# RMSNorm on one core: 19 transfers of x and out become 15, and two stores wait for a load

## The chip, the cores and the metric

The kernel runs on one core of a Trainium2 chip. The metric is the device time of one execution in microseconds (us), as the median of the runs. A profile of one execution shows what each engine did: PE (TensorE), DVE (VectorE), ACT (ScalarE), POOL (GpSimd), SP (SyncE, which here only issues transfers), and the core's 16 DMA engines.

## The reference

```
x: (16, 1024, 512) float32, gamma: (512,) float32
eps = 1e-5
rms = sqrt(mean(x ** 2, axis=-1, keepdims=True) + eps)
out = x / rms * gamma
```

Each of the 16,384 rows of 512 numbers is divided by its root mean square and multiplied by gamma. x has 33.55 MB and so has out; each byte crosses once.

## The kernel before

The rows are seen as 4 tiles of 128 partitions with 32 rows each (`xv`, `ov`: tile t, partition p, row r). One row over 128 partitions is 256 KB, one tile 8 MB. Three slots in SBUF hold a tile each: tiles 0 to 3 live in slots 0, 1, 2 and 0 again, so the loads of tile 3 overwrite rows of slot 0 that must have been stored. Results are written in place, into the slot.

A tile is worked in groups, `(tile, first row, rows, pieces of the squares, rows that POOL scales)`, listed in `groups` (L76). Tile 0 has three groups, (0,0) with 7 rows, (0,7) with 9 and (0,16) with 16; the others have two of 16. For each group:

- `square_sums` (L89): ACT squares a piece of rows into a scratch (L96), DVE sums each row of it (L97). A piece of 7 or 4 rows goes to PSUM (`sq_psum`), one of 5 to `sq_sbuf`. A piece of 9 rows goes to rows 23 to 32 of slot 2, which lie unused until tile 2 is loaded there.
- `inverse_rms` (L101): ACT takes the root (L102), DVE the reciprocal (L103).
- `scale_by_pool` (L106): POOL multiplies its share of the rows by the reciprocal (L109) and by gamma (L110).
- `scale` and `times_gamma` (L115, L120): for the other rows, ACT multiplies by the reciprocal, row by row (L118), and DVE by gamma (L122).

The main loop (L166) works one group ahead: the squares of the next group are recorded before the scaling of this one. The schedule is written by hand (`manual_schedule`): each engine runs its instructions in the order in which the code records them, and waits only where data demand it.

All transfers are issued by SP, in recorded order, to one queue: loads at L45, stores at L49, gamma at L58. An SP instruction that waits holds back all later ones. A transfer signals when it has landed. The first loads, of tile 0 and half of tile 1, are recorded ahead of the loop; the rest in `transfers` (L129), which is called after each group. Gamma is loaded in five pieces, spread over the partitions by a matmul (L66) and copied for POOL (L165).

The calls that the change touches stand after groups (0,0), (0,16) and (1,16). After (0,0), for instance, rows 0 and 1 of tile 0 are stored one at a time, between them the second half of tile 1 is loaded, and then rows 0 to 23 of tile 2, the part of slot 2 that holds no scratch. Rows 23 to 32 of tile 2 are loaded after (0,16), when the scratch has been read for the last time, by group (1,0), whose pieces are 7 and 9.

Of the kernel before, what the change touches and what calls it, by code (L numbers as in the profile page):

```python
# [9 lines left out]
def kernel(  # L10
# [15 lines left out]
    N, D = xf.shape  # L26
# [17 lines left out]
    def load(t, slot, r0, r1):  # L44
        dma = nc.sync.dma_start(out=slots[slot][:, r0:r1], in_=xv[t][:, r0:r1])  # L45
        before_scale.append((slot, r0, r1, dma))

    def store(t, slot, r0, r1):
        dma = nc.sync.dma_start(out=ov[t][:, r0:r1], in_=slots[slot][:, r0:r1])  # L49
        before_scale.append((slot, r0, r1, dma))  # L50

    gamma_row = const.tile([1, D], fp32)
    pieces = (0, 128, 224, 320, 416, D)

    load(0, 0, 0, 1)
    load(0, 0, 1, 8)
    for c0, c1 in zip(pieces, pieces[1:]):
        nc.sync.dma_start(out=gamma_row[:, c0:c1], in_=gamma.unsqueeze(0)[:, c0:c1])  # L58
    load(0, 0, 8, 16)
    load(0, 0, 16, 32)  # L60
    load(1, 1, 0, 16)

    ones_col = const.tile([1, P], fp32)
    nc.gpsimd.memset(ones_col, 1.0)  # L64
# [12 lines left out]
        (0, 0, 7, (7,), 3),  # L77
        (0, 7, 9, (9,), 5),
        (0, 16, 16, (7, 9), 7),
        (1, 0, 16, (7, 9), 7),  # L80
        (1, 16, 16, (7, 5, 4), 7),
        (2, 0, 16, (7, 5, 4), 7),
        (2, 16, 16, (7, 5, 4), 7),
# [36 lines left out]
    def times_gamma(t, g, r0, r1):  # L120
# [4 lines left out]
        for slot, b0, b1, earlier in before_scale:  # L125
            if slot == slot_of[t] and b0 < g + r1 and g + r0 < b1:
                tc.declare_no_dep(scaled.ins, earlier.ins, reason="ScalarE waited for it before it scaled these rows")

    def transfers(t, g):  # L129
        if (t, g) == (0, 0):  # L130
            store(0, 0, 0, 1)
            load(1, 1, 16, 32)
            store(0, 0, 1, 2)
            load(2, 2, 0, 23)
        elif (t, g) == (0, 16):
            store(0, 0, 2, 3)
            load(2, 2, 23, 32)
            store(0, 0, 3, 16)
            store(0, 0, 16, 32)
            load(3, 0, 0, 16)  # L140
            load(3, 0, 16, 32)
        elif (t, g) == (1, 16):
            store(1, 1, 0, 32)
        elif (t, g) == (2, 16):
            store(2, 2, 0, 32)
        elif (t, g) == (3, 0):
            store(3, 0, 0, 16)
        elif (t, g) == (3, 16):
            store(3, 0, 16, 32)
# [16 lines left out]
    for k, group in enumerate(groups):  # L166
        t, g, n, pieces, share = group
        mine = n - share
        half = (mine + 1) // 2
        ahead = groups[k + 1 :][:1]  # L170
        ss, todo = pieces_of(ahead[0]) if ahead else (None, [])
        scale_by_pool(rstd, t, g, n, share)
        for piece in todo[:2]:
            square_sums(*piece)
        scale(rstd, t, g, 0, half)
        for piece in todo[2:]:
            square_sums(*piece)
        scale(rstd, t, g, half, mine)
        times_gamma(t, g, 0, mine)
        transfers(t, g)  # L180
        for nxt in ahead:
            rstd = inverse_rms(ss, nxt[2])
# [30 lines left out]
```

## Time and profile before

| | before |
|---|---|
| median of 3 runs | 161.58 us (161.57 to 161.96) |
| profiled execution, span from first to last instruction | 160.2 us |
| bytes moved, mean rate over the span | 67.12 MB, 419 GB/s |
| busy DVE / ACT / POOL | 112.0 / 107.8 / 106.4 us |
| transfer engines busy | 98.1% of the span |
| end of the last compute instruction (DVE, L122) | 139.1 us |
| issue of the last store | 139.2 us |

The span is what the profile sees of one execution; a run's time is longer by what lies around it, 1.4 us here against the median. Busy times are sums over the span and say nothing of who waits for whom. Transfers are read in two ways: by the time from issue to landing, which holds the wait behind earlier transfers in the queue, and by the distance of two landings, which does not.

### The profile page before, as it was taken

Reading aid. Unit: us, or ns where it says so; the run is one execution under the profiler, and the core shown is the slowest. Engines: PE = TensorE matmul, PEld = TensorE weight load, DVE = VectorE, ACT = ScalarE, POOL = GpSimd, SP = SyncE. Lnnn points to the kernel's source line nnn. Section 1 sums busy time; section 2 is a strip of 40 time slices with the busy share of each in tenths; the row PEclk is TensorE's granted clock in tenths of the full one; section 3 lists DMA queues with packets and bytes.
Section 4 is the critical chain, followed back from the end, with each engine's and each line's share of the span. In section 5 each row is a group of like instructions: output and inputs, shape, how many; then the busy total and the mean of one; then the engine's idle time right before and its main releaser. Section 6 shows DMA issues by size and latency. Waiting matters only on the chain.

```text
span 160.2 us, 276 instructions
## 1 busy us (share of the span) xinstructions
PE 2.0 (1%) x2; PEld 0.5 (0%) x2; DVE 112.0 (70%) x39; ACT 107.8 (67%) x108; POOL 106.4 (66%) x24
## 2 busy tenths in 40 slices
PE   0050000000000000000000000000000000000000
PEld 0010000000000000000000000000000000000000
DVE  0018098899798999999999999999999009700000
ACT  3071967976999998999899899989960990000000
POOL 1000951994999599999999999999999980000000
DMA  5999999899999899999999999996996996999994
GB/s 189 431 421 475 442 401 458 340 446 491 417 435 494 388 379 383 426 450 475 434 401 426 483 401 393 524 491 295 524 491 295 524 491 295 401 491 417 401 450 196
DMA packets 2747, 67.12 MB, mean 419 GB/s; under 512 B 313, under 2 KB 314, under 8 KB 826
## 3 DMA queue, kind: packets, MB, share of 16 engines
q1 hardware_dynamic: 2746, 67.11, 98.1%
q14 instruction: 1, 0.01, 0.0%
HBM read 33.56 MB, written 33.55 MB: 419 GB/s over the span
## 4 chain that ended last, share of the span: by engine, by line
DVE 59%; ACT 22%; DMA 4%; ACTq 0%; issue 0%; SPq 0%
DVE ss L97 36%; DVE slot L122 23%; ACT slot L118 8%; ACT slot L96 7%; ACT sq_psum L96 6%; DMA slot<-in_x_dram 4%; DVE ss L103 1%; ACT ss L102 1%; ACTq L208 0%; ACT gamma_b L165 0%; SPq L45 0%; ACTq L96 0%
## 5 line engine op out<-in xcount | busy, mean ns | idle before, releaser
L109 POOL TENSOR_TENSOR slot<-slot,ss 128x3584 f32<-128x3584 f32 (+2 forms) x9 | 47.0, 5218 | 24.1 <-DVE ss L103 24.1
L110 POOL TENSOR_TENSOR slot<-slot,gamma_b 128x3584 f32<-128x3584 f32 (+2 forms) x9 | 59.3, 6587 | 0.7
L97 DVE TENSOR_REDUCE ss<-sq_psum 128x7 f32<-128x3584 f32 (+1 forms) x13 | 42.2, 3247 | 13.7 <-ACT sq_psum L96 13.7
L118 ACT ACTIVATE slot<-slot,ss 128x512 f32<-128x512 f32 x75 | 47.3, 706 | 4.7 <-DVE ss L103 4.7
L122 DVE TENSOR_TENSOR slot<-slot,gamma_psum 128x4608 f32<-128x4608 f32 (+2 forms) x9 | 41.3, 4590 | 8.7 <-ACT slot L118 8.7
L96 ACT ACTIVATE sq_psum<-slot 128x3584 f32<-128x3584 f32 (+1 forms) x13 | 34.6, 2658 | 6.4 <-DMA slot<-in_x_dram 5.7
L97 DVE TENSOR_REDUCE ss<-slot 128x9 f32<-128x4608 f32 x3 | 14.9, 4954 | 4.4 <-ACT slot L96 4.2
L97 DVE TENSOR_REDUCE ss<-sq_sbuf 128x5 f32<-128x2560 f32 x5 | 14.0, 2803 | 0.0
L96 ACT ACTIVATE slot<-slot 128x4608 f32<-128x4608 f32 x3 | 12.1, 4033 | 0.0
L96 ACT ACTIVATE sq_sbuf<-slot 128x2560 f32<-128x2560 f32 x5 | 11.6, 2321 | 0.0
L102 ACT ACTIVATE ss<-ss,eps_t 128x16 f32<-128x16 f32 (+2 forms) x9 | 2.7, 305 | 11.9 <-DVE ss L97 11.9
L103 DVE RECIPROCAL ss<-ss 128x16 f32<-128x16 f32 (+2 forms) x9 | 2.1, 236 | 0.4 <-ACT ss L102 0.4
L66 PE MATMUL gamma_psum<-gamma_row,ones_col 1*128 1x512 f32 x2 | 2.0, 1122 | 8.6 <-DMA gamma_row<-in_gamma_dram 8.6
L72 ACT ACT_TABLE_LOAD x1 | 1.3, 1283 | 1.2 <-PEq L197 1.2
L165 ACT COPY gamma_b<-gamma_psum 128x512 f32<-128x512 f32 x1 | 0.6, 567 | 0.0
L66 PEld LDWEIGHTS gamma_psum<-gamma_row,ones_col 1*128 1x128 f32 x2 | 0.5, 308 | 8.6 <-issue 8.6
L64 POOL MEMSET ones_col<- 1x128 f32 x1 | 0.2, 195 | 0.3 <-POOLq L197 0.3
L197 POOL MEMSET const-float32-0.0<- 128x1 f32 x1 | 0.1, 99 | 0.2 <-issue 0.2
L72 ACT ACTIVATE table<-eps_t 128x1 f32<-128x1 f32 x1 | 0.2, 202 | 0.0
L197 POOL MEMSET const-bfloat16-1.0<- 128x1 bf16 x1 | 0.1, 102 | 0.0
L197 POOL MEMSET const-uint8-127<- 128x1 uint8 x1 | 0.1, 102 | 0.0
L197 POOL MEMSET const-float32-1.0<- 128x1 f32 x1 | 0.1, 99 | 0.0
(1 smaller groups left out, 0.1 us busy)
## 6 DMA issues: line engine op xcount, KB each, us to landing
slot<-in_x_dram SPq DMA_DIRECT2D x5, 4096.0 KB, 21.9
out_dram<-slot SPq DMA_DIRECT2D x3, 4096.0 KB, 23.4
slot<-in_x_dram SPq DMA_DIRECT2D x1, 5888.0 KB
out_dram<-slot SPq DMA_DIRECT2D x1, 3328.0 KB, 21.8
slot<-in_x_dram SPq DMA_DIRECT2D x1, 2304.0 KB, 14.3
slot<-in_x_dram SPq DMA_DIRECT2D x1, 2048.0 KB, 9.9
slot<-in_x_dram SPq DMA_DIRECT2D x1, 1792.0 KB, 7.0
out_dram<-slot SPq DMA_DIRECT2D x3, 256.0 KB
```

What stands on the lines that cost most here:

```text
L66: nc.tensor.matmul(gamma_psum[:, 0], ones_col, gamma_row, start=True, stop=True)
L72: nc.scalar.activation(out=table, in_=eps_t, func=AF.Sqrt)
L96: nc.scalar.activation(out=sq[:, :m], in_=rows, func=AF.Square)
L97: nc.vector.tensor_reduce(out=ss[:, r : r + m, 0], in_=sq[:, :m], axis=mybir.AxisListType.X, op=OP.add)
L102: nc.scalar.activation(out=ss[:, :n, 0], in_=ss[:, :n, 0], func=AF.Sqrt, bias=eps_t, scale=1.0 / D)
L103: nc.vector.reciprocal(out=ss[:, :n, 0], in_=ss[:, :n, 0])
L109: nc.gpsimd.tensor_tensor(out=part, in0=part, in1=by_row, op=OP.mult)
L110: last = nc.gpsimd.tensor_tensor(out=part, in0=part, in1=gamma_b.to_broadcast([P, share, D]), op=OP.mult)
L118: nc.scalar.activation(out=x[:, g + r, :], in_=x[:, g + r, :], func=AF.Copy, scale=rstd[:, r])
L122: scaled = nc.vector.tensor_tensor(out=part, in0=part, in1=gamma_psum.to_broadcast([P, r1 - r0, D]), op=OP.mult)
L165: nc.scalar.copy(out=gamma_b[:, 0], in_=gamma_psum[:, 0])
L197: nc = _bacc.Bacc("TRN2", target_bir_lowering=False, num_devices=1)
```

## The change

The one-row stores of tile 0 go, and loads and stores are cut differently:

| | before | after |
|---|---|---|
| tile 0 in | rows 0:1, 1:8, 8:16, 16:32 | 0:8, 8:32 |
| gamma | 5 pieces | 1 piece |
| tile 1 in | 0:16 at the start, 16:32 after (0,0) | 0:16, 16:32, both at the start |
| tile 2 in | 0:23 after (0,0), 23:32 after (0,16) | 0:30, 30:32, both after (0,7) |
| tile 0 out | 0:1 and 1:2 after (0,0), 2:3, 3:16, 16:32 after (0,16) | 0:16, 16:32 after (0,16) |
| tile 3 in | 0:16, 16:32 | 0:16, 16:30, 30:32 |
| tile 1 out | 0:32 | 0:32 |
| tile 2 out, tile 3 out | 0:32; 0:16, 16:32 | the same |

Two stores get a wait that their data do not ask for: tile 0's rows 0:16 are issued when the load of tile 2's rows 0:30 has landed, and tile 1's when the load of tile 3's rows 16:30 has. The squares of group (1,0) are cut into pieces of 7, 5 and 4 rows in place of 7 and 9; the last reader of the scratch in slot 2 is then group (0,16).

```diff
-    def store(t, slot, r0, r1):
+        return dma
+
+    def store(t, slot, r0, r1, behind=None):
         dma = nc.sync.dma_start(out=ov[t][:, r0:r1], in_=slots[slot][:, r0:r1])
+        if behind is not None:
+            tc.add_manual_dep(
+                dma.ins,
+                behind.ins.name,
+                mybir.DependencyInfo(mybir.DependencyClass.Sync, mybir.DependencyReason.DATA),
+                reason="the store is issued when this load has landed",
+            )
         before_scale.append((slot, r0, r1, dma))
...
-    pieces = (0, 128, 224, 320, 416, D)
+    pieces = (0, D)
 
-    load(0, 0, 0, 1)
-    load(0, 0, 1, 8)
+    load(0, 0, 0, 8)
     for c0, c1 in zip(pieces, pieces[1:]):
         nc.sync.dma_start(out=gamma_row[:, c0:c1], in_=gamma.unsqueeze(0)[:, c0:c1])
-    load(0, 0, 8, 16)
-    load(0, 0, 16, 32)
+    load(0, 0, 8, 32)
     load(1, 1, 0, 16)
+    load(1, 1, 16, 32)
...
-        (1, 0, 16, (7, 9), 7),
+        (1, 0, 16, (7, 5, 4), 7),
...
+    late = {}
+
     def transfers(t, g):
-        if (t, g) == (0, 0):
-            store(0, 0, 0, 1)
-            load(1, 1, 16, 32)
-            store(0, 0, 1, 2)
-            load(2, 2, 0, 23)
+        if (t, g) == (0, 7):
+            late[2] = load(2, 2, 0, 30)
+            load(2, 2, 30, 32)
         elif (t, g) == (0, 16):
-            store(0, 0, 2, 3)
-            load(2, 2, 23, 32)
-            store(0, 0, 3, 16)
+            store(0, 0, 0, 16, behind=late[2])
             store(0, 0, 16, 32)
             load(3, 0, 0, 16)
-            load(3, 0, 16, 32)
+            late[3] = load(3, 0, 16, 30)
+            load(3, 0, 30, 32)
         elif (t, g) == (1, 16):
-            store(1, 1, 0, 32)
+            store(1, 1, 0, 32, behind=late[3])
```

## The prediction

> **What bounds the kernel now.** I read the page's DMA rows first, because 67 MB pass through one core, then the SP rows of the timeline (every transfer is issued there), then the DMA issues with their time to landing, and last the chain of waits.
>
> The row of slices for the transfer engines, and the queue's row (packets, MB, share of 16 engines):
>
> ```profile
> DMA  5999999899999899999999999996996996999994
> ...
> q1 hardware_dynamic: 2746, 67.11, 98.1%
> ```
>
> One queue carries everything and its 16 engines hardly pause between the first and the last slice. DVE, ACT and POOL are busy 70, 67 and 66%. The last compute instruction (DVE, L122) ends at 139.1 and the span at 160.2, so 21 us at the end are transfers alone. The transfer engines are the bound: time is bytes at a fixed rate plus every pause of the queue. The chain view on the page names DVE for 59%, but it only follows the work that released the last store; that store waited behind others (20.1 us from issue to landing, of which its own data takes half).
>
> The SP rows of the timeline (start, length and number of issues):
>
> ```profile
> 0.74 0.86 SPq L45 DMA_DIRECT2D slot<-in_x_dram  x2
> ...
> 3.17 5.39 SPq L45 DMA_DIRECT2D slot<-in_x_dram  x3
> ...
> 28.69 0.43 SPq L45 DMA_DIRECT2D slot<-in_x_dram  x1
> ...
> 49.83 0.33 SPq L45 DMA_DIRECT2D slot<-in_x_dram  x1
> 50.25 5.48 SPq L49 DMA_DIRECT2D out_dram<-slot  x2
> 72.09 10.27 SPq L45 DMA_DIRECT2D slot<-in_x_dram  x2
> 83.64 55.90 SPq L49 DMA_DIRECT2D out_dram<-slot  x4
> ```
>
> and one row of SP's waits (total, times, longest):
>
> ```profile
> SPq L208 <- DMA out_dram<-slot: 19.6, 3, 9.6
> ```
>
> SP always issues well ahead of need. The first load of tile 2 is issued at 28.69, while loads issued before it land until 43.1 (completion events). The last 9.6 us wait is one 16-row store: a row of 128 partitions (256 KB) costs 0.604 us (completion events 149.67 and 159.34: 9.67 for 16 rows). 256 rows cost 154.7 us; the other 4.6 us before the last landing are start-up and small losses.
>
> Time to landing of three loads at the start (size, us):
>
> ```profile
> slot<-in_x_dram SPq DMA_DIRECT2D x1, 256.0 KB, 2.9
> ...
> slot<-in_x_dram SPq DMA_DIRECT2D x1, 1792.0 KB, 7.0
> ...
> slot<-in_x_dram SPq DMA_DIRECT2D x1, 4096.0 KB, 24.5
> ```
>
> They were issued at 0.74, 1.18 and 8.24 and landed at 3.6, 8.2 and 32.8. The last is 16 rows, 9.67 us of data, and took 24.5: it landed 9.95 after the load issued before it (22.83), so the queue serves in order of issue, one transfer after the other.
>
> And from the chain, the piece of it that the change will lean on:
>
> ```profile
> 16.20 3.95 ACT slot L96
> ...
> 25.47 3.04 ACT sq_psum L96
> 28.51 3.97 ACT slot L96
> ...
> 32.51 4.96 DVE ss L97
> ```
>
> From the start of the 9-row square of (0,7) at 16.20 to the end of the second 9-row reduce at 37.46 there are 21.26 us in which ACT and DVE wait for each other step by step, none of it for a transfer.
>
> **The change, part by part.** Times below are landings; the span ends 0.83 us after the last (159.34 to 160.17), and the median 161.58 is 1.41 above the span.
>
> *The price of a restart.* In the trace before, the queue runs dry only at the start, so that is the nearest row. Issue at 0.74, eight rows landed at 8.22: 7.48 less 8 x 0.604 leaves 2.65 us. That is the upper end, since it includes the one-row transfer's 2 KB packets (117 ns mean there, 84 ns in mid-run). Lower end: first packet at 1.75, so 1.0 after issue, and 0.35 from last packet to landing (158.99 to 159.34): 1.35, which is the quickest engine's case and not the slowest's. I take the middle, 2.0. Below 1.35 nothing can go, because both pieces are seen; a store may restart differently from a load, and no row shows it.
>
> The Trainium skill, "DMA: Bandwidth & Descriptors", section "Latency and other measured facts", gives about 0.6 us to the first byte for SP's path; by an estimate from that figure a restart would cost 0.95 and not 2.0, the first pause below 2.7 us, the other two nothing, and the sum would be 163.5. The trace's 1.0 us to the first packet differs from it, and the trace decides.
>
> *Load of rows 8 to 32 in one piece.* The 9-row square needs rows 8 to 16. Before, they had landed at 13.1 and the square began at 16.20. Now it waits for all 24 rows: x(0, 0:8) at about 7.8, plus 24 x 0.604, is 22.3. So the whole compute chain moves by 6.1 us.
>
> *Load of tile 2 moved past the scratch.* Before, rows 0 to 23 of slot 2 were loaded from 28.69, free of the scratch in rows 23 to 32. Now the load of rows 0 to 30 is issued after (0,7) and overwrites the scratch, so on SP it waits for the second 9-row reduce (the instruction order has it wait for DVE's seventh). That is 21.26 us after the square: 22.3 + 21.3 + 0.05 = 43.6. What is queued ahead by then: x(1, 0:16) and x(1, 16:32), 2 x 9.67 plus the 0.28 that the first of them lost before, so the queue is empty at 22.3 + 19.6 = 41.9. The load restarts it: 43.6 + 2.0 - 41.9 = **3.7 us of pause** (3.1 to 4.4). This does not depend on when the 24 rows land, as both sides start from it. Behind the waiting load on SP stand the 2-row load and the stores of tile 0; no engine waits for these in this time.
>
> *The stores behind a load.* The store of rows 0 to 16 used to be issued at 50.25 while loads ran until 64.1. Now SP holds it until x(2, 0:30) has landed; covered only by the two remaining rows, 1.21 us. Pause: 0.05 + 2.0 - 1.21 = 0.84 (0.2 to 1.5). The store of tile 1, before at 83.64 with some 17 us of loads ahead of it, waits the same way for x(3, 16:30): 0.84 again. **Together 1.7 us** (0.4 to 3.0). Its scale work is long done (POOL ends (1,16) at 83.6 before, 90 now; the landing is at 103). Behind it on SP is the store of tile 2, whose rows are done at 118, before 125 when the tile 1 store lands.
>
> *Fewer transfers.* The three one-row stores took 0.64, 0.67 and 0.64 between landings, against 0.604 by bytes: 0.14 in all. x(2, 23:32) took 5.78 against 5.44: 0.34. The new 2-row loads cost about 0.05 each, by the one-row stores. Net gain 0.4 (0 to 0.8).
>
> The Trainium skill speaks for this part: on the same page, section "Rules for kernel authors", many small transfers are to be made into one large one, and the section "Anatomy of one DMA" fits, for transfers issued by GpSimd, a fixed 2.0 us to each. Eight transfers fewer (24 to 16, gamma's included) would by an estimate from that fit be worth up to 16 us, if nothing hid it, and the sum would fall far below 161.58. In this full queue the trace gives a one-row transfer 0.07 us over its bytes at most.
>
> *Start.* One transfer of eight rows in place of 1 + 7, four gamma pieces fewer: the small packets go, 8.2 becomes about 7.8. Gain 0.4 (0 to 0.7).
>
> *Three pieces for (1,0) in place of 7 + 9*: the reduces become 2.80 + 2.28 against 4.95, the squares 2.32 + 1.88 against 4.03; the scale is then split around a square. About 0.5 us more on the chain, hidden: with the 6.1 us shift the last DVE instruction ends at about 146, and the store before it lands at 154, so the last store still has 6 us to spare beyond the restart's 2.0. Were that cover gone, it would be a fourth pause. The loads of tile 3 wait for tile 0's stores as before, each with a 16-row transfer in front, and land at 95 and 105; their squares begin at about 98 and 112.
>
> Sum: +3.7 + 1.7 - 0.4 - 0.4 = **+4.6 us**, 161.58 + 4.6 = **166.2 us**.
>
> **The rivals.**
> 1. *The tile 2 load is not late.* If ACT and DVE made up the shift, or the load were issued before 41.9 - 2.0 = 39.9, only the store pauses are left: 161.58 + 1.7 - 0.8 = 162.5. Against it: the 21.26 us hold no wait for a transfer that could shrink, and the waited-for reduce is named in the order.
> 2. *Faster: the queue never runs dry.* The transfers' losses go and every issue is in time: 161.58 - 0.8 = 160.8, at best 160.1. One mechanism would decide it: an issue must reach the engines within the 1.21 us of the two tail rows, and the first pause must vanish as in rival 1. For it: the first packet came 1.0 us after the issue. Against it: landing adds 0.35, and the first pause is 3 us away from zero.
> 3. *Restarts cost what the start cost, 2.65.* Pauses 4.4 + 2 x 1.5 and no gains: 161.58 + 7.4 = 169.0, with the forecast's gains 168.2.
> 4. *The wait does less than it says*, passing when only some engines have landed: the order has it wait for all 16 counts, so I give it no share of its own; it would save the store pauses, 164.5.
>
> **How the numbers follow.** Forecast (three pauses, 164 to 168) 0.84; rival 3 beyond 168 0.07; rival 1 0.05; rival 2 0.04. Bounds of the forecast: low 161.58 + 3.5 - 1.5 = 163.6, high 169.0; eight in ten go to 164.3 to 167.9. A difference of 0.3% (0.5 us) is about what a measurement of this kernel can tell from no change. Faster has rival 2 less its weakest edge, 0.03; same 0.03, between rivals 1 and 2; slower 0.94.
>
> **What would show it.** The SP rows should have the tile 2 load issued at 43 to 44 after a wait for DVE's reduce, and the DMA row a slice or two of low share at 41 to 46, shorter dips near 65 and 105, and 9s elsewhere. ACT should wait some 6 us for a transfer at its second square, and the last store should be issued near 146 and still wait behind another. I am wrong if the load is issued before 40, if the share at 41 to 46 stays full, if the dips at the stores last over 1.5 us each, or if the last store finds the queue empty.

## The result, and the profile after

The changed kernel takes 167.52 us (167.31 to 167.99, 4 runs) against 161.73 for the kernel before on the same chip: 1.0361 times as long, 95% interval 1.0336 to 1.0385, +5.8 us. The forecast was 166.2, range 164.3 to 167.9.

The page's DMA slices and queue row, after:

```profile
DMA  6989988988569996899899999999599599798985
...
q1 hardware_dynamic: 2162, 67.11, 95.4%
```

SP's rows of the timeline, after (start, length, issues):

```profile
1.53 43.35 SPq L45 DMA_DIRECT2D slot<-in_x_dram  x5
65.00 0.82 SPq L50 DMA_DIRECT2D out_dram<-slot  x2
76.24 11.46 SPq L45 DMA_DIRECT2D slot<-in_x_dram  x3
105.22 40.99 SPq L50 DMA_DIRECT2D out_dram<-slot  x4
```

SP's waits, after (total, times, longest):

```profile
SPq L45 <- DVE ss L104: 41.1, 1, 41.1
SPq L50 <- DMA slot<-in_x_dram: 37.4, 2, 20.0
...
SPq L45 <- DMA out_dram<-slot: 20.6, 2, 10.3
```

The same bytes pass in 5.5 us more of span, and the queue's share falls from 98.1 to 95.4%. The long wait for L104 is the one that matters: the load of tile 2, in the first row the fourth of five issues, is held until 44.07 by DVE's reduce. SP waited for a reduce in the kernel before as well:

```profile
SPq L45 <- DVE ss L97: 20.1, 1, 20.1
```

That was the load of tile 2's last nine rows, issued at 49.83 while earlier transfers were still landing until 58.35, so the wait cost nothing there. The two waits of L50 for a load are the held stores. The two 5s in the DMA row at 116 and 128 us are no pauses: a packet's time counts in the slice in which it starts, the stores' 64 KB packets take 2.42 us each and start together on all 16 engines, and a slice of 4.1 us holds one or two such rounds. The store of tile 2, served from 126 to 145, loses only 0.07 us. The windows around 44.07 show the queue empty (columns: length, the engines' busy time, granted clock, share of the transfer engines, GB/s; again a packet's whole time counts where it starts, so 2.89 only means that all 16 engines begin again):

```profile
40.00:41.00 1.00, 0.00 (x0) 0.00 (x0) 1.00 (x1) 1.00 (x3) 1.00 (x1) 1.00 0.99 426
41.00:42.00 1.00, 0.00 (x0) 0.00 (x0) 1.00 (x1) 0.51 (x1) 1.00 (x1) 1.00 0.01 0
42.00:43.00 1.00, 0.00 (x0) 0.00 (x0) 1.00 (x1) 0.00 (x0) 1.00 (x1) 1.00 0.00 0
43.00:44.00 1.00, 0.00 (x0) 0.00 (x0) 1.00 (x2) 0.00 (x0) 1.00 (x1) 1.00 0.00 0
44.00:45.00 1.00, 0.00 (x0) 0.00 (x0) 1.00 (x2) 0.92 (x2) 0.23 (x1) 1.00 0.00 0
45.00:46.00 1.00, 0.00 (x0) 0.00 (x0) 1.00 (x1) 1.00 (x1) 0.00 (x0) 1.00 2.89 983
```

DVE is busy right through it: the engines are not waiting for the load, the load waits for them. The cause lies one step earlier, in ACT's wait for the 24-row load, and in the chain that starts from it:

```profile
ACT slot L103 <- DMA slot<-in_x_dram: 6.7, 1, 6.7
```

```profile
22.67 4.05 ACT slot L103
...
35.09 3.98 ACT slot L103
...
39.09 4.96 DVE ss L104
```

The square that began at 16.20 begins at 22.67, and the reduce that ended at 37.46 ends at 44.05.

Since the queue serves in order, the time goes into segments: from one landing (the completion events) to the next, less 0.604 us for each row. What is left over, in us:

| segment | before | after |
|---|---|---|
| to the landing of the first 8 rows | 3.38 | 3.20 |
| rest of tile 0 and tile 1 in (before: two one-row stores among them) | 0.48 | 0.18 |
| tile 2 in (before: one one-row store) | 0.42 | 4.75 |
| tile 0 out, to row 16 | 0.08 | 0.34 |
| tile 0 out, rows 16:32 | 0.26 | 1.03 |
| tile 3 in | -0.05 | 0.13 |
| tile 1 out | 0.05 | 0.34 |
| tile 2 and tile 3 out | -0.02 | 0.10 |
| sum | 4.60 | 10.07 |

4.72 of tile 2's 4.75 belong to the late load. The 1.03 at the second store of tile 0 was in nobody's sum. A further 0.2 us lies outside the span: runs of the kernel before spend 1.7 to 1.8 us around it, the changed kernel 1.9 to 2.0.

### The profile page after: what moved, and what is told of

Same layout as the page of the kernel before. It is cut to its first block, busy times and chain, and to the rows that moved or that the text cites. A ratio compares the mean times of both kernels' runs of the same rounds, so it can differ in the third digit from the quotient of the medians.

```text
span 165.6 us, 264 instructions
## 1 busy us (share of the span) xinstructions
PE 2.0 (1%) x2; PEld 0.5 (0%) x2; DVE 112.1 (68%) x40; ACT 108.1 (65%) x109; POOL 106.3 (64%) x24
## 3 DMA queue, kind: packets, MB, share of 16 engines
q1 hardware_dynamic: 2162, 67.11, 95.4%
## 4 chain that ended last, share of the span: by engine, by line
DVE 55%; ACT 19%; DMA 13%; SPq 0%; ACTq 0%; issue 0%
DVE ss L104 32%; DVE slot L129 22%; DMA slot<-in_x_dram 13%; ACT slot L125 8%; ACT slot L103 5%; ACT sq_psum L103 5%; ACT sq_sbuf L103 1%; DVE ss L110 1%; ACTq L214 0%; ACT ss L109 0%; SPq L45 0%; SPq L65 0%
## 5 line engine op out<-in xcount | busy, mean ns | idle before, releaser
L104 DVE TENSOR_REDUCE ss<-sq_psum 128x7 f32<-128x3584 f32 (+1 forms) x14 | 44.5, 3179 | 13.9 <-ACT sq_psum L103 13.9
L103 ACT ACTIVATE sq_psum<-slot 128x3584 f32<-128x3584 f32 (+1 forms) x14 | 36.4, 2602 | 6.1 <-DMA slot<-in_x_dram 5.4
L104 DVE TENSOR_REDUCE ss<-slot 128x9 f32<-128x4608 f32 x2 | 9.9, 4954 | 11.1 <-ACT slot L103 11.0
L104 DVE TENSOR_REDUCE ss<-sq_sbuf 128x5 f32<-128x2560 f32 x6 | 16.8, 2803 | 0.0
L103 ACT ACTIVATE sq_sbuf<-slot 128x2560 f32<-128x2560 f32 x6 | 13.9, 2321 | 0.0
L103 ACT ACTIVATE slot<-slot 128x4608 f32<-128x4608 f32 x2 | 8.1, 4035 | 6.7 <-DMA slot<-in_x_dram 6.7
```

The lines of the kernel that those rows point to most:

```text
L103: nc.scalar.activation(out=sq[:, :m], in_=rows, func=AF.Square)
L104: nc.vector.tensor_reduce(out=ss[:, r : r + m, 0], in_=sq[:, :m], axis=mybir.AxisListType.X, op=OP.add)
```

## The experiments

Twelve kernels; each is told by its difference from the kernel before on the same chip, since the chips differ by 0.2 us. The middle column is the difference of two medians; the ratio is not their quotient and differs from it by up to 0.16%.

| kernel | median, us | over before | ratio, 95% interval |
|---|---|---|---|
| changed kernel | 167.52 | 5.79 | 1.0361 (1.0336 to 1.0385) |
| e1, tile 2 early | 163.18 | 1.69 | 1.0107 (1.0094 to 1.0120) |
| e2, 8:16 and 16:32 | 163.10 | 1.61 | 1.0098 (1.0085 to 1.0111) |
| e3, no store held | 168.14 | 6.65 | 1.0415 (1.0402 to 1.0428) |
| e4, tile 2 early, no store held | 163.44 | 1.95 | 1.0115 (1.0096 to 1.0133) |
| e5n, as e4, no 2-row loads | 162.08 | 0.43 | 1.0016 (0.9998 to 1.0035) |
| e5, as e1, no 2-row loads | 165.14 | 3.49 | 1.0200 (1.0159 to 1.0241) |
| e6, as e4, a load held | 165.49 | 3.84 | 1.0230 (1.0180 to 1.0280) |
| h1, as e5n, first store held | 164.66 | 3.12 | 1.0192 (1.0179 to 1.0205) |
| h2, as e5n, second store held | 163.66 | 2.12 | 1.0132 (1.0118 to 1.0147) |
| e8, before without one-row stores | 162.08 | 0.43 | 1.0016 (0.9990 to 1.0042) |
| s1, before with the new start | 161.76 | 0.22 | 1.0014 (1.0006 to 1.0023) |
| t1, before with a 2-row load | 162.42 | 0.88 | 1.0064 (1.0047 to 1.0082) |

**Is it the late load, and what makes it late?** e1 starts from the changed kernel:

```diff
-        if (t, g) == (0, 7):
-            late[2] = load(2, 2, 0, 30)
+        if (t, g) == (0, 0):
+            load(2, 2, 0, 23)
+        elif (t, g) == (0, 7):
+            late[2] = load(2, 2, 23, 30)
             load(2, 2, 30, 32)
```

> The changed kernel with rows 0 to 23 of tile 2 loaded right behind tile 1 (they hold no scratch), and only rows 23 to 30 and 30 to 32 loaded after group (0,7). Everything else, the two held stores too, as in the changed kernel. Theory A (the queue ran dry because the tile 2 load waited on SP for DVE's reduce, 4.72 us between landings over its bytes): that pause goes, 167.5 - 4.7 = 162.8 us, 162.3 to 163.3. Theory B (the loss comes from holding the two stores back, whatever the load does): within 1 us of 167.5.

e2 leaves the tile 2 load where it is and gives the square its rows early:

```diff
-    load(0, 0, 8, 32)
+    load(0, 0, 8, 16)
+    load(0, 0, 16, 32)
```

> The changed kernel with rows 8 to 32 of tile 0 loaded in two transfers, 8:16 and 16:32, as before; the tile 2 load still waits for the scratch. Theory A: the second square starts at about 16 and not at 22.67, the reduce that the tile 2 load waits for ends at about 37.5 and not at 44.0, some 4 us before the queue would run dry at 42; the pause goes and the time is that of the kernel with the early tile 2 load, 162.8 us (162.3 to 163.3). Theory B: within 1 us of 167.5. Were the place of the tile 2 load the whole cause, and not the late square, the time would also stay near 167.5.

Both remove it: 4.1 us in e1, 4.2 in e2, each within its expected range, and in neither trace does the queue pause before tile 2. In e2's timeline SP has issued all loads of tiles 0 to 2 by 38.2, the held one at 37.40, while tile 1 lands until 42.2:

```profile
1.55 36.65 SPq L45 DMA_DIRECT2D slot<-in_x_dram  x6
```

So the pause needed both edits: the 24-row load that made the reduce late, and the 30-row load that waits for it. Theory B, that holding stores is the loss, falls. The waiting of a load on SP is harmless by itself too: in e1 rows 23 to 30 wait until 43.86, while the load ahead of them lands until 56.0.

**What do the held stores cost?** e3 is the changed kernel and e4 is e1, each with these edits:

```diff
-            store(0, 0, 0, 16, behind=late[2])
+            store(0, 0, 0, 16)
...
-            store(1, 1, 0, 32, behind=late[3])
+            store(1, 1, 0, 32)
```

> The changed kernel without the two waits of stores for loads: the stores are issued as soon as their rows are done. The trace of the changed kernel has 0.34 us over the bytes at each held store, so theory A expects 167.5 - 0.7 = 166.8 us (166.3 to 167.1); the prediction's own price of 0.84 each would give 165.8. Theory B expects most of the 5.8 us back, 162 to 163.

> Both: rows 0 to 23 of tile 2 loaded early, and no store held for a load. What is left of the change is fewer transfers, no one-row stores, one start transfer, one gamma piece, and three pieces for group (1,0). Theory A: no pause is left, 167.5 - 4.7 - 0.7 = 162.1 us by the trace's terms; the prediction's credits (0.8 below the kernel before) would make it 160.9. If the one-row stores and small pieces cost nothing that lasts, it is the kernel before, 161.7, within 0.3.

Both missed: without the holds the time does not fall by 0.7. It rises by 0.9 in e3 (against the changed kernel); in e4 it is 0.3 over e1, where the two intervals overlap. The completion events say where: with the store queued behind it, the 2-row load of tile 2 takes 2.27 us in e3, against 1.24 in the changed kernel (1.21 by bytes), and that of tile 3 takes 2.32 in e4 against 1.26 in e1. From the changed kernel to e3, the loads in front of the two stores lose 2.0 us more and the stores themselves 1.4 us less. So the holds cost something and saved at least as much. The 2-row loads are then the suspects. e5n is e4 without them:

```diff
-            late[2] = load(2, 2, 23, 30)
-            load(2, 2, 30, 32)
+            late[2] = load(2, 2, 23, 32)
...
-            late[3] = load(3, 0, 16, 30)
-            load(3, 0, 30, 32)
+            late[3] = load(3, 0, 16, 32)
```

> As the kernel with the early tile 2 load and no held stores, but without the 2-row loads: tile 2 in rows 0:23 and 23:32, tile 3 in 0:16 and 16:32. Its sister with 2-row loads took 163.4 us, 1.9 over the kernel before, and its trace has 1.0 us over the bytes at each of the two places where a 2-row load is followed by a waiting store. Theory C (a 2-row load, 4 KB packets, is slowed by the store queued behind it): the switches cost some 0.4 each, as in the kernel before, 163.4 - 1.3 = 162.1 us, 161.6 to 162.4. Theory D (the one-row stores of the kernel before did good by themselves, since they stood between loads): it stays near 163.4.

162.08, in the range of theory C; D falls. The agreement hides an error of C, though. It expected a gain at both places, and the traces show it at one: the end of tile 3 loses 0.19 in place of 1.16 us, but the last nine rows of tile 2 lose 0.82 in one piece and 0.79 in two. Another 0.36 of the gain lies around the span. t1 puts one 2-row load into the kernel before, and nothing else:

```diff
-            load(3, 0, 16, 32)
+            load(3, 0, 16, 30)
+            load(3, 0, 30, 32)
```

> The kernel before, with tile 3's rows 16:32 loaded as 16:30 and 30:32; the store of tile 1 is queued behind them as before. Theory C (a 2-row load is slowed by a store queued behind it): the two loads take 0.7 to 1.1 us more between landings than the one did, 162.4 to 162.8 us. The prediction's price of a short transfer, 0.05: no difference, 161.7. The time around the span was 1.76 in kernels without 2-row loads and 1.9 to 2.1 in those with them; if the 2-row load is the cause it is about 1.9 here.

It costs 0.88 us, as theory C expected: the last two rows land in 1.88 us, where bytes ask for 1.21, and 1.94 us lie around the span, against 1.77 in the kernel before on that chip. All seven kernels with a 2-row load have 1.9 to 2.1 there (medians) and all others 1.74 to 1.79; why a 2-row load shows up outside the span stays open.

**What does a restart cost?** e5 is e1 with the same whole loads and both stores still held, so that no row is left in the queue to cover the restart:

> The kernel with the early tile 2 load (163.2 us), its two held stores now held for the whole load (tile 2's rows 23:32, tile 3's rows 16:32): no row is left in the queue to cover the restart. By the trace a held store landed 1.48 us over its bytes after its issue. If that is the price of a store's restart, each pause grows from 0.34 to 1.5: 163.2 + 2.3 = 165.5 us. If the price is that of a queue that has run dry, 2.7 as at the tile 2 load, each grows to 2.75: 163.2 + 4.8 = 168.0.

e6 is e4 with a load held behind two rows of cover (`load` gets the same `behind` as `store`):

```diff
-    load(1, 1, 16, 32)
+    first = load(1, 1, 16, 30)
+    load(1, 1, 30, 32)
...
-            load(2, 2, 0, 23)
+            load(2, 2, 0, 23, behind=first)
```

> The kernel with the early tile 2 load and no held stores (163.4 us), with one load held: tile 1's rows 16:32 are loaded as 16:30 and 30:32, and tile 2's rows 0:23 are issued when rows 16:30 have landed, so a load restarts behind two rows of cover. If a restart costs 2.7 because it is a load: 2.75 - 1.21 = 1.5 us of pause, 164.9. If it cost 2.7 only because the queue was dry, and behind cover costs 1.5 like the stores: 0.3, 163.8.

Issue to landing: the late load and the first held store of the changed kernel, then the first held store of e5, then the held load of e6.

```profile
slot<-in_x_dram SPq DMA_DIRECT2D x1, 7680.0 KB, 20.9
```

```profile
out_dram<-slot SPq DMA_DIRECT2D x1, 4096.0 KB, 11.2
```

```profile
out_dram<-slot SPq DMA_DIRECT2D x1, 4096.0 KB, 11.1
```

```profile
slot<-in_x_dram SPq DMA_DIRECT2D x1, 5888.0 KB, 16.3
```

Less 0.604 a row, from the completion events: a store restarts in 1.46 to 1.50 us behind cover and 1.44 to 1.46 in an empty queue (e5, h1, h2), a load in 2.44 behind cover and 2.72 in an empty queue (3.04 in e3, where a store was queued behind that load before it ended). So e5 came out near the 165.5 us of a store's own price, and far from 168.0. It is the direction that counts, far more than the cover. The size of the packets is not the reason: the eight rows at the start of the eleven kernels that load them in one piece have packets of 16 KB, smaller than a store's, and landed 2.37 to 2.62 us over their bytes after their issue. The first packets show where a part of it lies: in the changed kernel the first 60 KB packet of 15 of the 16 engines after the pause takes longer than by its bytes, by 0.66 us in the median, while the first 32 KB packets of the held store lose 0.02. Why a load's first packets are slow stays open. e6 misses its 164.9 by 0.6: its pause is 1.23, less than was expected, but its 2-row load ahead of the tile 0 store takes 2.81, against 1.50 in e4.

**Where does the 1.03 at the second tile 0 store come from?** It stands in all four kernels with the first store held so far (changed, e1, e2, e5: 1.01 to 1.05) and in none without (0.07 to 0.43 in before, e3, e4, e5n, e6, e8, s1 and t1). h1 and h2 hold one store each, behind whole loads:

> The kernel with whole loads and early tile 2 (162.08 us, nothing held), with only the store of tile 0's rows 0:16 held, until the load of tile 2's rows 23:32 has landed. Theory E (a held store also makes the next switch, from the second tile 0 store to the tile 3 load, cost about 1 us, because all 16 engines leave the pause in step and then switch in step): pause 1.5, the slow end of the load (0.8) gone, the dear switch 0.95 in place of 0.1: 162.1 + 1.5 - 0.8 + 0.85 = 163.7 us, and the second store of tile 0 takes 10.7 between landings. Theory F (that store's 10.7 has nothing to do with the hold of the store before it): 162.8, and the store takes 9.9.

> The same, with only the store of tile 1 held, until the load of tile 3's rows 16:32 has landed. No load follows this store, so theory E has only the pause, 1.5 less the 0.2 that the end of that load loses otherwise: 163.4 us, and the second store of tile 0 takes 9.9 between landings. Theory F: 163.4 too if that store is not slow here, 164.3 with 10.7 for it.

SP's wait for tile 0's two stores, which slot 0's next loads need, in h1 and in h2:

```profile
SPq L45 <- DMA out_dram<-slot: 20.6, 2, 10.3
```

```profile
SPq L45 <- DMA out_dram<-slot: 19.3, 2, 9.7
```

The store takes 10.70 us between landings in h1 and 10.02 in h2: the hold of the first store does it, F falls; h2's time, 163.66, is near the 163.4 expected. In h1 the last packet of that store, on all 16 engines at once, is 0.78 us longer on average than by its bytes, just before the tile 3 load follows. h1 came out 1.0 over its expectation, and the trace has that too: the load of tile 3's rows 16:32, with the unheld tile 1 store behind it, takes 10.79 in place of e5n's 9.86. So in h1 both later switches of direction after the one hold cost 1 us. The reason given, that the engines leave the pause in step, fits the completion events (the 16 engines finish the first store within 0.19 us in h1, 0.50 in h2, 0.53 in e5n), but the spread was not changed by itself, so it is argued and not shown.

**Do the credits exist?** These are the gains that the prediction counted for fewer transfers and for the start. e8 is the kernel before with its one-row stores merged into the next store, s1 the kernel before with one 8-row load and one gamma piece.

```diff
-            store(0, 0, 0, 1)
...
-            store(0, 0, 1, 2)
...
-            store(0, 0, 2, 3)
...
-            store(0, 0, 3, 16)
+            store(0, 0, 0, 16)
```

> The kernel before, with the three one-row stores taken out and tile 0's rows 0:16 stored in one; all else as it was. Prediction's term: one-row stores cost 0.14 us in all, so 161.3 to 161.5. Theory C says the same, within 0.3 of the kernel before. Theory D: slower than the kernel before by 1 us or more.

```diff
-    load(0, 0, 0, 1)
-    load(0, 0, 1, 8)
+    load(0, 0, 0, 8)
...
-    pieces = (0, 128, 224, 320, 416, D)
+    pieces = (0, D)
```

> The kernel before, with tile 0's rows 0:8 in one load and gamma in one piece. The prediction's credit for the start: 0.4 us, 161.2. The traces so far show the eight rows landing at 7.94 to 8.19 against 8.22: gain 0.1 to 0.2, no difference that can be measured, 161.5.

Neither gains anything. e8 is 0.4 over the kernel before, with an interval that takes in no difference, and s1 0.2 over it, just clear of no difference. In e8's trace the one-row stores' own losses are gone, but the load in front of the tile 0 store now ends slowly (6.28 us between landings for 5.44 of bytes, 5.78 in the kernel before). None of the twelve beats the kernel before; s1, e8 and e5n come nearest.

## Why the prediction was right, and which of its sizes were off

- **The bound and the first pause: right, too small.** The load was issued at 44.07 (43.6 forecast) into a queue empty since 42.07 (41.9). ACT's wait was 6.7 us (some 6). The pause was 4.72, not 3.7, above even the upper bound of 4.4. Two terms: the load was 2.0 late and not 1.7, partly since tile 1 landed in 19.42 us and not in 19.6 (the 0.28 that was carried over is found in the three traces where a one-row store follows that load, before, t1 and s1, with 0.28 to 0.43, and in no other); and the restart cost 2.72, not 2.0. The step that failed is the middle between 1.35 and 2.65: the upper end was the row of a load from an empty queue, which this is, and should have been taken. The changed kernel's own start, one transfer of eight rows without the small packets, still landed 2.47 us over its bytes. The prediction's 1.0 us from issue to first packet is counted from the start of SP's instruction, which takes 0.38 us; from its end it is 0.63, and 0.58 at the late load, so the trace does not contradict the 0.6 us that the prediction set against it. The 0.95 worked out from it left out those 0.38 us and the slow first packets.
- **The held stores: mechanism half right.** 0.34 each and not 0.84, because a store restarts in 1.5. The step "a store may restart differently from a load" was left at one price for both. What it missed altogether: the first hold makes a later switch dear (1.03 in place of 0.26), and a hold also saves the slow end of a 2-row load, so taking the holds away gains nothing.
- **Fewer transfers: wrong.** The 0.34 at x(2, 23:32) was not the price of a short transfer: the same nine rows take 5.49 in e5, where no store is issued behind them before they land, and 6.25 to 6.33 in e5n, e8 and h2, where one is. But with a store queued behind them they also took 5.49 in t1 and 5.68 in s1, so the queued store alone does not set the loss. In t1, s1 and the kernel before, a one-row store runs just ahead of the nine rows; no run tests whether that is the reason. The 0.14 for the one-row stores is real between landings, but removing them gains nothing (e8). The new 2-row loads were priced at 0.05 by one-row stores; in front of a waiting store one costs 0.7 in the queue (t1).
- **Start: half the size at most.** 8.04 against 8.22, 0.2 and not 0.4 in the traces, and nothing in s1.
- **Three pieces for (1,0): right as far as the trace shows; no run tests them alone.** The last DVE instruction ends at 145.8, the last store is issued at 145.87 and lands 18.9 us later, 9.7 of it its own data.
- **The offset around the span.** The 1.41 set the profiled execution's span against the median; runs of the kernel before that list both have 1.7 to 1.8, so that execution was one of the slower. Only the difference was forecast, which this does not touch.
- **The sum.** 4.6 against 5.8 measured. Too low: 1.0 at the first pause, 0.8 for the dear switch and 0.2 around the span, both left out. Too high: 1.0 at the held stores. The credits of 0.8 have a counterpart in the table, 0.7 over all the rest. But e8 and s1, which make the edits of the one-row stores and of the start alone, show none of it in the time, and some 0.2 of the 0.7 is only that the profiled execution of the kernel before was one of the slower. So the sum came within its range by its main term, the late load, and with errors that happened to offset each other in part, which was luck. Rivals 1 and 2 fell with the load at 44.07; rival 3's 2.65 held for loads alone. Rival 4 fell too: the two held stores were issued 0.08 and 0.13 us after the last of the 16 completion events of the load that they wait for.
- The Trainium skill, "DMA: Bandwidth & Descriptors", section "Anatomy of one DMA", fits a fixed 2.0 us for transfers issued by GpSimd. The restarts here, issued by SP, lie on both sides of it, 1.44 to 1.50 for stores and 2.44 to 3.04 for loads. Its section "Rules for kernel authors" wants small transfers made into large ones, those under 64 KB above all. e5n has 14 transfers of x and out and one of gamma in place of 24; of the nine fewer, only gamma's four were that small, and the others were of 256 KB and more. It is 0.4 us over the kernel before, with an interval that takes in no difference, so in this queue, which is always full, the merging brought nothing.

## What to carry to other kernels

When one transfer queue is the bound, look for the time at which it runs empty, not for the number of transfers: write down for each load when it is issued and when the queue ahead of it ends, and include what the issuing instruction now waits for. Merging two loads moves the first use of the early rows to the landing of the last, and merging a load over a scratch makes it wait for the scratch's last reader; neither emptied the queue here without the other. Price a restart by direction, and a wait put on a store by what it does to the transfers after it too.

## What the runs showed of the hardware that was not expected

- A load restarts in 2.44 to 2.72 us over its bytes (3.04 in e3), a store in 1.44 to 1.50, from issue to landing.
- A 2-row load (4 KB packets) with a store queued behind it takes 1.5 to 2.8 us for 1.21 us of bytes; with the transfer behind it held until the load in front of it has landed, 1.22 to 1.27.
- After a held store, the next switch from stores to loads costs 1 us (10.7 for 9.67 us of bytes), and in h1 the next from loads to stores 1.1; without a hold the same switches left 0.07 to 0.43 and, behind whole loads, 0.05 to 0.2.
- The last nine rows of tile 2, with a store queued behind them, take 5.49 to 6.33 us for 5.44 of bytes; what decides it stays open.
- Kernels with a 2-row load have 0.15 to 0.35 us more around the span (seven kernels; why stays open).
